# A table of its own for layer B's attention, and every table of orders and steps dealt out anew, in a two-layer encoder kernel

## The chip, the cores and the metric

The kernel runs on one core of one Trainium2 chip. The metric is the device time of one execution in microseconds (us), taken as the median of several executions. Five engines work side by side: TensorE (PE in the profile; its weight loads are PEld), VectorE (DVE), ScalarE (ACT), GpSimd (POOL) and SyncE (SP), which here only issues DMA transfers; POOL issues some too.

## The reference

An input of 256 frames by 2048 features in float32 passes two layers. Cut to what matters:

```python
h = x
u = rms_norm(h, a_norm_g)                      # layer A
q, k, v, fz = split(u @ a_w_in)                # 16 heads of 128
o = forgetting_attention(rms_norm(q), rms_norm(k), v, log_sigmoid(fz + a_b_f))   # causal
h = h + o @ a_w_out
h = h + relu(rms_norm(h, g1) @ w1_A)**2 @ w2_A # d_ff = 8192
kv = rms_norm(h, kv_norm_g) @ kv_w             # keys and values for layer B, computed once
k_sh, v_sh = rms_norm(kv[:, :2048]), kv[:, 2048:]
q = rms_norm(rms_norm(h, b_norm_g) @ b_w_q)    # layer B
o = chunked_relbias_attention(q, k_sh, v_sh, b_rel)   # chunks of 64, own and 8 before
h = h + o @ b_w_out
h = h + relu(rms_norm(h, g2) @ w1_B)**2 @ w2_B
```

All weights are float32 and are read once from memory.

## The kernel before

**Split in two.** A float32 product is made of three products of rounded parts. Each weight block of 128 x 1024 is loaded raw (L295, buffer `raw`, three of them, 1 MB each in the MLPs), ACT rounds it to `hi` (L310), DVE takes the rest as `lo` = raw - hi (L319), and PE multiplies: hi with the activations' high part (L628), hi with their low part (L630), lo with their high part (L632). So every block passes ACT, then DVE, then PE. Four pairs of `hi` and `lo` buffers are there (AHEAD + 2).

**Forms.** The MLPs and layer B's query projection are cut into pairs. An MLP has four chunks of 2048 hidden features, and each chunk has four pairs: `w10`, `w11` (columns of w1) and `w20`, `w21` (columns of w2, which add into the residual `h`). In a pair, part of the contraction is done by seven products of sums instead of eight plain ones: forms f0 to f6, on the weights 11, T3, T2, T1, 21, T4, 22 in this order, each in two halves of 6 matmuls (f0.0 and f0.1 and so on). The rest are plain products: items a4 to a7 and b4 to b7 of 12 matmuls each. The blocks 11 and 12 are brought whole, 1 MB each, into buffers of their own (`bring`, L337, printed w), and turned in place into T3 and T1 by accumulating DMAs that POOL issues (L350). T2 is a sum made on DVE (`make`, L357, tile wT); T4 is T2 plus 21, again on DVE in two halves (L348), and 21 is a raw block, whose buffer is free for the next load when L348 has read it. Between the forms DVE combines accumulators: L673 after f2 (it needs f1's copy p, made by ACT at L671), L675 after f3. f3 writes over the accumulator that L673 reads; a4 and f4 add to the one that it writes.

**Orders and steps.** PE's order is written out in ORDER, one string for each kind of pair, where `r` takes an item that the pair before left over (`first` is the first pair of an MLP, `w20+` and `w21+` are the last two). What the other engines do, and in which order, follows from tables:

- `fetch` (L378) runs before each item: it makes `lo` blocks until LOOK of them are ready, `hi` blocks until MORE further, and loads as far as the raw buffers go.
- BEHIND hangs `make`, `add` (T4 on DVE; T1, T3 as DMAs) and `bring` behind a form; the first number is a delay, counted in `lo` blocks.
- HIDDEN, LONG, SHORT, QUERY, AGAIN, ATT and BIAS say at which step a piece of work is run that belongs to no weight block: `run_fill` takes one step after each item. HIDDEN deals out the squared ReLU of a block of hidden features, LONG and SHORT the norm and transposition of the residual, QUERY and AGAIN layer B's queries and the second use of the turned residual for keys and values, ATT and BIAS an attention group.

A transposition takes DVE's 32 x 32 blocks (L475, tile z) and 16 small DMAs (`moves`, L490, q<-z), eight issued by SP and eight by POOL; ACT then scales the result (L451 for normed inputs, tile y; L990 for hidden features). For heads, `head_norm` squares on ACT (L719) and norms on DVE (L731), the turn goes through memory (land<-turn), and L754 scales what has landed.

At the end `keep_order` fixes the order of DVE, ACT, PE and SP as written; POOL's order is left to the scheduler. A wait thus holds up everything that was written behind it on its engine, SP's transfers included.

The lines that fix it:

```python
def fetch(ahead=AHEAD, early=EARLY, more=0):
    while (units or raws or highs) and len(ready) <= ahead:
        low()
    while (units or raws) and len(ready) + len(highs) <= ahead + more and can_high():
        high()
    while units and sum(r[3] for r in raws) < early:
        load()
    return ready.popleft()
```

Of the kernel before, what the change touches and what calls it, by code (L numbers as in the profile page):

```python
# [29 lines left out]
EARLY = 4  # L30
MINI = 0
HIDDEN = (
# [4 lines left out]
)  # L37
UA = UN // 512
LONG = (
# [4 lines left out]
)  # L44
SHORT = (
# [4 lines left out]
)  # L50
REL = 384
QUERY = (0, 1, 14, 10, 3, 15, 3)
AGAIN = (0, 1, 2, 3, 5, 5, 7, 7)
ATT = ((8, 14, 18, 18, 10), (8, 8, 12, 12, 9))
BIAS = (3, 6, 7)
LOOK = {
# [6 lines left out]
}  # L63
MORE = {
# [6 lines left out]
}  # L71
ORDER = {
# [9 lines left out]
}  # L82
BEHIND = {
    "w10": {(0, 0): [(0, 1, "make", 0), (7, 1, "add", "T1", 0)], (0, 1): [(3, 1, "add", "T1", 1), (0, 1, "make", 1)], (1, 1): [(1, 0, "bring", "12", 0), (1, 0, "bring", "12", 1)], (3, 1): [(6, 0, "bring", "11", 0), (5, 0, "bring", "11", 1)], (4, 0): [(1, 1, "add", "T4", 0)], (4, 1): [(0, 1, "add", "T4", 1), (9, 0, "add", "T3", 1)], (6, 0): [(0, 0, "add", "T3", 0)]},
    "w11": {(0, 0): [(0, 1, "make", 0), (7, 1, "add", "T1", 0)], (0, 1): [(2, 1, "add", "T1", 1), (0, 1, "make", 1)], (1, 1): [(1, 0, "bring", "12", 0), (1, 0, "bring", "12", 1)], (3, 1): [(5, 0, "bring", "11", 0), (7, 0, "bring", "11", 1)], (4, 0): [(0, 1, "add", "T4", 0)], (4, 1): [(0, 1, "add", "T4", 1), (10, 0, "add", "T3", 1)], (6, 0): [(2, 0, "add", "T3", 0)]},
    "w20": {(0, 0): [(7, 1, "add", "T1", 0), (0, 1, "make", 0)], (0, 1): [(0, 1, "make", 1)], (1, 1): [(0, 0, "bring", "12", 0), (0, 0, "bring", "12", 1), (3, 1, "add", "T1", 1)], (3, 1): [(5, 0, "bring", "11", 0), (2, 0, "bring", "11", 1)], (4, 0): [(1, 1, "add", "T4", 0)], (4, 1): [(0, 1, "add", "T4", 1), (8, 0, "add", "T3", 1)], (6, 0): [(0, 0, "add", "T3", 0)]},
    "w21": {(0, 0): [(0, 1, "make", 0), (7, 1, "add", "T1", 0)], (0, 1): [(0, 1, "make", 1), (1, 1, "add", "T1", 1)], (1, 1): [(2, 0, "bring", "12", 1)], (3, 1): [(5, 0, "bring", "11", 0)], (4, 0): [(1, 1, "add", "T4", 0)], (4, 1): [(0, 1, "add", "T4", 1), (9, 0, "add", "T3", 1), (5, 0, "bring", "11", 1)], (5, 0): [(0, 0, "add", "T3", 0)], (2, 1): [(1, 0, "bring", "12", 0)]},
    "q0": {(0, 0): [(0, 1, "make", 0), (7, 1, "add", "T1", 0)], (0, 1): [(3, 1, "add", "T1", 1), (0, 1, "make", 1)], (1, 1): [(1, 0, "bring", "12", 0), (1, 0, "bring", "12", 1)], (3, 1): [(5, 0, "bring", "11", 0), (4, 0, "bring", "11", 1)], (4, 0): [(1, 1, "add", "T4", 0), (0, 0, "add", "T3", 0)], (4, 1): [(0, 1, "add", "T4", 1), (10, 0, "add", "T3", 1)]},
    "q1": {(0, 0): [(0, 1, "make", 0), (8, 1, "add", "T1", 0)], (0, 1): [(5, 1, "add", "T1", 1), (0, 1, "make", 1)], (1, 1): [(1, 0, "bring", "12", 0), (1, 0, "bring", "12", 1)], (3, 1): [(7, 0, "bring", "11", 1), (5, 0, "bring", "11", 0)], (4, 0): [(1, 1, "add", "T4", 0)], (4, 1): [(0, 1, "add", "T4", 1), (10, 0, "add", "T3", 1)], (6, 0): [(0, 0, "add", "T3", 0)]},
}  # L90
SUBS = {"1": (2, 2), "2": (2, 2), "q": (2, 2)}
OPENING = (
    (18, "bring", "12", 0),
    (16, "bring", "12", 1),
    (9, "add", "T3", 0),
    (5, "add", "T3", 1),
    (4, "bring", "11", 0),
    (12, "bring", "11", 1),
)
BIG = 2 * UN  # L100
FORMS = ("11", "T3", "T2", "T1", "21", "T4", "22")
# [14 lines left out]
def trunk(ctx: ExitStack, tc: tile.TileContext, t):  # L116
# [706 lines left out]
    def attend(g, q, k, v, cq, o, make_bias):  # L823
        st = [{} for _ in range(GH)]
        box = {}
        k4 = k.rearrange("p (i a b c) -> p a b i c", i=4, a=GH, b=NB)
        *at, far = ATT[g == NG - 1]
        items = [[] for _ in range(at[-1] + far + 1)]
        step = steps(lambda: make_bias(g, box))
        for i in BIAS:  # L830
            items[i].append(step)
        for a in range(GH):
            step = steps(lambda a=a: softmax(st[a], g, a, q(), k4, box["b"], cq() if cq else None))
            for i in range(4):
                items[at[a] + i].append(step)
            items[at[a] + 3].append(lambda a=a: add_fill(st[a]["carry"]))
            items[at[a] + far].append(lambda a=a: values(st[a], a, v, o, g * GH + a))
        return items
# [220 lines left out]
                            p.evac[q](b, p.ps[q][b])  # L1059

    if MINI:
        for i in range(H):
            o[i] = quarter(i)
            if i % GH == 0:
                G.memset(part[0].bitcast(F32), 0.0)
# [32 lines left out]
    if MINI:  # L1098
        keep_order(tc, (V.engine, S.engine, TE.engine, SY.engine))
        return  # L1100

# [20 lines left out]

    st3, x3, S3 = RowStats("n"), [], []
    stage(o, [next_x(n, None, st3, 4, x3, fs=S3, then=st3.inverse if n == NG - 1 else None) for n in range(NG)], tail=tail_b, plan=plan_b)

    def store(n, r2):
        add_h = residual(n, r2)
# [74 lines left out]
```

## Time and profile before

| | us |
|---|---|
| median of 3 executions | 2114.33 |
| lowest and highest | 2112.9 and 2116.64 |
| the profiled execution | 2111.67 |
| its span, first to last instruction | 2109.9 |
| PE busy | 2073.8 (98%) |
| DVE busy | 1722.0 (82%) |
| ACT busy | 1292.4 (61%) |
| POOL busy | 354.8 (17%) |

The granted TensorE clock was 0.998 over the span, and the kernel moved 538.89 MB at 255 GB/s. In order of time: layer A's projections and attention (to about 340 us), its output projection (to about 386), MLP A (386 to 1053), the query pairs q0 and q1 (1053 to 1141), keys, values and attention of layer B (to 1386), its output projection (to 1430), MLP B (to the end). In the profile a row of a timeline gives start, duration, engine, line, operation, and in brackets how long the engine had been idle and what released it; a matmul row counts several matmuls, and their step is read from the starts of rows that follow each other.

### The profile page before, as it was taken

What the parts mean: (1) busy time and instruction counts of PE and PEld (TensorE: products, weight loads), DVE (VectorE), ACT (ScalarE), POOL (GpSimd) and SP (SyncE); (2) the same over time, 40 slices, a digit from 0 to 9 for tenths busy, and PEclk for the clock granted to TensorE, in tenths of its full rate; (3) what the DMA queues carried; (4) which work ended last, traced back from release to release, by engine and by line L of the source; (5) the groups of instructions that cost most, each with busy time, mean ns of one, the idle gap of its engine ahead of it and who ended that gap; (6) DMA issues with size and microseconds to landing.
All of it is one profiled execution on the core that took longest, in us unless ns stands there. A gap on an engine that the chain in (4) does not pass through costs nothing.

```text
span 2109.9 us, 26958 instructions
## 1 busy us (share of the span) xinstructions
PE 2073.8 (98%) x9114; PEld 1698.1 (80%) x9114; DVE 1722.0 (82%) x2003; ACT 1292.4 (61%) x1567; POOL 354.8 (17%) x552
## 2 busy tenths in 40 slices
PE   9999999999999999999999999999999999999999
PEld 7888888787887887887777888887878878878877
DVE  6777775898889889889998667768988898898896
ACT  6544545676667567567676445456765665675674
POOL 1001001231031022022213001022300310220220
PEclk9999999999999999999999999999999999999999
DMA  8777778899789898888886767778988898888884
GB/s 302 242 257 225 238 245 260 264 263 285 258 267 247 269 285 249 253 276 268 253 246 223 249 212 249 235 249 262 281 272 260 258 263 269 272 254 258 272 262 165
DMA packets 160635, 538.89 MB, mean 255 GB/s; under 512 B 42848, under 2 KB 68080, under 8 KB 125680
## 3 DMA queue, kind: packets, MB, share of 16 engines
q1 hardware_dynamic: 129136, 453.78, 61.1%
q0 software_dynamic: 31360, 83.39, 21.1%
q8 instruction: 71, 1.16, 0.2%
q14 instruction: 68, 0.56, 0.1%
HBM read 497.20 MB, written 15.75 MB: 243 GB/s over the span
## 4 chain that ended last, share of the span: by engine, by line
PE 73%; DMA 10%; DVE 9%; issue 4%; ACT 3%; SPq 1%; DVEq 0%; ACTq 0%; POOL 0%; POOLq 0%
PE acc L628 16%; PE acc L632 16%; PE acc L630 16%; DVE lo L319 6%; PE po L628 4%; PE po L632 4%; PE po L630 4%; PE s L632 3%; PE s L630 3%; PE s L628 3%; DMA w<-in_f2b 2%; DMA w<-in_f2a 2%; ACT hi L310 2%; DMA q<-z 1%; SPq L490 1%
## 5 line engine op out<-in xcount | busy, mean ns | idle before, releaser
L319 DVE TENSOR_TENSOR lo<-raw,hi 128x1024 fp32r<-128x1024 f32 (+1 forms) x634 | 752.8, 1213 | 144.3 <-ACT hi L310 134.3
L310 ACT ACTIVATE hi<-raw 128x1024 fp32r<-128x1024 f32 (+1 forms) x634 | 655.3, 1053 | 309.1 <-PE acc L630 131.5
L628 PE MATMUL acc<-hi,act 128*128 128x512 f32 x1644 | 457.3, 394 | 6.2 <-ACT hi L310 3.3
L632 PE MATMUL acc<-lo,act 128*128 128x512 f32 x1644 | 449.3, 390 | 1.2 <-DVE lo L319 1.2
L630 PE MATMUL acc<-hi,act 128*128 128x512 f32 x1644 | 449.7, 390 | 0.0
L628 PEld LDWEIGHTS acc<-hi,act 128*128 128x128 f32 x1644 | 307.2, 188 | 73.4 <-ACT hi L310 6.6
L632 PEld LDWEIGHTS acc<-lo,act 128*128 128x128 f32 x1644 | 308.3, 188 | 68.1 <-DVE lo L319 3.7
L630 PEld LDWEIGHTS acc<-hi,act 128*128 128x128 f32 x1644 | 309.1, 188 | 65.4 <-DVE act L421 0.5
L310 ACT ACTIVATE hi<-w 128x1024 fp32r<-128x1024 f32 x204 | 210.8, 1054 | 110.6 <-PE po L630 30.3
L319 DVE TENSOR_TENSOR lo<-w,hi 128x1024 fp32r<-128x1024 f32 x204 | 243.5, 1218 | 42.2 <-ACT hi L310 42.0
L490 POOL DMA_DIRECT2D q<-z x336 | 170.4, 529 | 255.2 <-DVE z L475 97.8
L319 DVE TENSOR_TENSOR lo<-wT,hi 128x1024 fp32r<-128x1024 f32 x136 | 161.3, 1218 | 17.7 <-ACT hi L310 17.2
L310 ACT ACTIVATE hi<-wT 128x1024 fp32r<-128x1024 f32 x136 | 141.2, 1052 | 50.7 <-DVE wT L348 26.8
L628 PE MATMUL s<-hi,act 128*128 128x512 f32 x476 | 136.2, 391 | 1.7 <-ACT hi L310 1.6
L630 PE MATMUL s<-hi,act 128*128 128x512 f32 x476 | 135.9, 390 | 0.7 <-DVE act L1001 0.7
L632 PE MATMUL s<-lo,act 128*128 128x512 f32 x476 | 136.0, 390 | 0.6 <-DVE lo L319 0.5
L628 PEld LDWEIGHTS s<-hi,act 128*128 128x128 f32 x476 | 89.4, 188 | 21.7 <-ACT hi L310 2.9
L632 PEld LDWEIGHTS s<-lo,act 128*128 128x128 f32 x476 | 89.1, 188 | 20.4 <-DVE lo L319 1.9
L630 PEld LDWEIGHTS s<-hi,act 128*128 128x128 f32 x476 | 89.2, 188 | 20.2 <-DVE act L1001 1.6
L727 POOL TENSOR_TENSOR rn<-vv,mhalf 128x4 f32<-128x4 f32 x32 | 44.1, 1391 | 341.8 <-DVE vv L726 341.8
L350 POOL DMA_DIRECT2D w<-in_f1a x32 | 28.6, 967 | 324.6 <-ACT hi L310 113.2
L357 DVE TENSOR_TENSOR wT<-w,w 128x1024 f32<-128x1024 f32 x68 | 82.9, 1219 | 0.0
(183 smaller groups left out, 2333.9 us busy)
## 6 DMA issues: line engine op xcount, KB each, us to landing
raw<-in_w_in SPq DMA_DIRECT2D x94, 512.0 KB, 5.2
raw<-in_s1a SPq DMA_DIRECT2D x32, 1024.0 KB, 6.9
raw<-in_s2a SPq DMA_DIRECT2D x32, 1024.0 KB, 7.7
raw<-in_w_kv SPq DMA_DIRECT2D x64, 512.0 KB, 5.8
raw<-in_s1b SPq DMA_DIRECT2D x32, 1024.0 KB, 6.8
raw<-in_s2b SPq DMA_DIRECT2D x32, 1024.0 KB, 5.9
raw<-in_w_oa SPq DMA_DIRECT2D x32, 512.0 KB, 6.1
w<-in_f1a SPq DMA_DIRECT2D x16, 1024.0 KB, 7.0
```

Source lines behind the costliest of these rows:

```text
L310: S.activation(hi[:, c], raw[:, c], AF.Copy)
L319: V.tensor_tensor(lo[:, c], raw[:, c], hi[:, c].bitcast(F32), op=ALU.subtract)
L350: G.dma_start(d, p.big[block][:, half(s)], accum_op=ALU.add)
L357: V.tensor_tensor(p.t["T2"][:, half(s)], p.t["T3"][:, half(s)], p.t["11"][:, half(s)], op=ALU.add)
L490: (SY, G)[j % 2].dma_start(d[32 * j : 32 * j + 32, i], z[32 * i : 32 * i + 32, j * n : (j + 1) * n])
L628: TE.matmul(ps, xh, cut(hi, j), start=first, stop=False, **kw)
L630: TE.matmul(ps, xl, cut(hi, j), start=False, stop=False, **kw)
L632: TE.matmul(ps, xh, cut(lo, j), start=False, stop=last, **kw)
L727: G.tensor_tensor(rn, vv, mhalf, op=ALU.pow)
```

## The change

Every table is given new numbers, ATT and BIAS get entries of their own for layer B (before, both layers used the same), and one line of DMA steps (OPENING) is moved. No instruction of the computation is added or removed. The diff, cut to the entries that the prediction speaks of and the code:

```diff
-QUERY = (0, 1, 14, 10, 3, 15, 3)
-AGAIN = (0, 1, 2, 3, 5, 5, 7, 7)
-ATT = ((8, 14, 18, 18, 10), (8, 8, 12, 12, 9))
-BIAS = (3, 6, 7)
+QUERY = (0, 1, 13, 10, 5, 9, 3)
+AGAIN = (0, 0, 1, 3, 4, 4, 7, 5)
+ATT = ((8, 14, 18, 18, 10), (8, 8, 12, 12, 9), (8, 13, 18, 18, 10), (8, 8, 12, 12, 8))
+BIAS = ((3, 6, 7), (3, 6, 4))
...
 ORDER = {
-    "first": "r f0 r f1 r r r f2 f3 r a a r f4 f6 r b f5 a a b",
+    "first": "r f0 r f1 r r f2 r a f3 a r r f4 f6 r f5 b a a b",
...
-    "w11": "f0 f1 r f2 r r f4 a f3 r a a r r f5 a f6 b b",
-    "w20": "r f0 r f1 f2 f4 r f3 f5 a r a f6 b r r",
+    "w11": "f0 f1 r f2 r r r f4 f3 a a a r r f5 a f6 b b",
+    "w20": "r f0 r f1 f2 f4 r f3 f5 a r r a b f6 r",
...
 BEHIND = {
...
-    "w20": {... (4, 0): [(1, 1, "add", "T4", 0)], (4, 1): [(0, 1, "add", "T4", 1), (8, 0, "add", "T3", 1)], ...},
+    "w20": {... (4, 0): [(2, 1, "add", "T4", 0)], (4, 1): [(0, 1, "add", "T4", 1), (8, 0, "add", "T3", 1)], ...},
...
-        *at, far = ATT[g == NG - 1]
+        *at, far = ATT[2 * (cq is None) + (g == NG - 1)]
...
-        for i in BIAS:
+        for i in BIAS[cq is None]:
```

What moves is read from the instructions' order on each engine. Below, rows with - stand in the kernel before, rows with + in the changed one; the numbers in names like w_5660 only tell buffers apart and differ between the two.

**Pair w20, DVE.** In the pair w20 of the second chunk of MLP A, around f2, f4 and f3 (from 639 us in the trace), DVE's order; the same stands in all eight w20 pairs:

```order
 L319 TENSOR_TENSOR lo<-wT_5427,hi 128x1024 x2
 L319 TENSOR_TENSOR lo<-raw,hi 128x1024 x2
-L348 TENSOR_TENSOR wT_5427<-wT_5427,raw 128x1024 x2
+L348 TENSOR_TENSOR wT_5427<-wT_5427,raw 128x1024
 L673 TENSOR_TENSOR s<-p_5548,po 128x512
-L319 TENSOR_TENSOR lo<-w_5317,hi 128x1024 x2
+L319 TENSOR_TENSOR lo<-w_5300,hi 128x1024
+L348 TENSOR_TENSOR wT_5427<-wT_5427,raw 128x1024
+L319 TENSOR_TENSOR lo<-w_5300,hi 128x1024
 L319 TENSOR_TENSOR lo<-wT_5427,hi 128x1024 x2
 L675 TENSOR_TENSOR po<-po,p_5548 128x512
```

The second half of T4's sum has moved behind L673 and behind one more lo.

**Pair w20, SP.** SP's order in the same pair; w_5660 is block 11 of the pair behind it, w21, and the f in in_f2a marks blocks for the forms, the s those for plain products:

```order
 L490 DMA q<-z 32x256 x8
 L337 DMA w_5505<-in_f2a 128x2048
-L295 DMA raw<-in_f2a 128x2048
-L490 DMA q<-z 32x256 x2
-L295 DMA raw<-in_s2a 128x2048
+L295 DMA raw<-in_s2a 128x2048
+L490 DMA q<-z 32x256 x2
+L295 DMA raw<-in_f2a 128x2048
 L490 DMA q<-z 32x256 x6
 L337 DMA w_5660<-in_f2a 128x2048
```

The two raw loads have changed places; the one right ahead of the six moves is in both cases the one whose buffer L348's second half sets free.

**The first pair of an MLP, ACT.** From the copy p (L671, 386 us in MLP A) on, ACT before:

```order
L671 ACTIVATE p_3433<-po 128x512
L310 ACTIVATE hi<-wT_3309 128x1024
L310 ACTIVATE hi<-w_3228 128x1024 x2
L451 ACTIVATE y<-q,gsb 128x256 x2
L454 ACTIVATE act<-y 128x1024
L310 ACTIVATE hi<-raw 128x1024 x7
L451 ACTIVATE y<-q,gsb 128x256 x4
L454 ACTIVATE act<-y 128x1024
L310 ACTIVATE hi<-wT_3309 128x1024 x2
```

and after:

```order
L671 ACTIVATE p_3433<-po 128x512
L451 ACTIVATE y<-q,gsb 128x256 x2
L454 ACTIVATE act<-y 128x1024
L310 ACTIVATE hi<-wT_3309 128x1024
L310 ACTIVATE hi<-raw 128x1024
L310 ACTIVATE hi<-w_3220 128x1024 x2
L310 ACTIVATE hi<-raw 128x1024 x5
L310 ACTIVATE hi<-wT_3309 128x1024
L451 ACTIVATE y<-q,gsb 128x256 x4
L454 ACTIVATE act<-y 128x1024
L310 ACTIVATE hi<-wT_3309 128x1024
L310 ACTIVATE hi<-raw 128x1024 x4
```

Of the hi blocks before the four L451 one is now of wT_3309 (for f5), and the raw block of b4 stands behind the group; in the kernel before both blocks for f5 stood behind it. The same holds in MLP B.

**Start of the keys and values, ACT.** ACT from the last inputs for keys and values (L451, 1140 us) on, before:

```order
L451 ACTIVATE y<-land,gsb 128x256 x4
L454 ACTIVATE act<-y 128x1024
L310 ACTIVATE hi<-raw 128x1024
L719 ACTIVATE sq<-acc 128x512 x2
L310 ACTIVATE hi<-raw 128x1024
L754 ACTIVATE q<-land,gqk 128x1024
L310 ACTIVATE hi<-raw 128x1024
L754 ACTIVATE q<-land,gqk 128x1024 x2
L310 ACTIVATE hi<-raw 128x1024 x6
L719 ACTIVATE sq<-acc 128x512 x2
L310 ACTIVATE hi<-raw 128x1024 x8
L754 ACTIVATE q<-land,gqk 128x1024
```

and after:

```order
L310 ACTIVATE hi<-raw 128x1024
L451 ACTIVATE y<-land,gsb 128x256 x2
L454 ACTIVATE act<-y 128x1024
L310 ACTIVATE hi<-raw 128x1024
L754 ACTIVATE q<-land,gqk 128x1024
L719 ACTIVATE sq<-acc 128x512 x2
L310 ACTIVATE hi<-raw 128x1024 x2
L754 ACTIVATE q<-land,gqk 128x1024
L310 ACTIVATE hi<-raw 128x1024 x2
L754 ACTIVATE q<-land,gqk 128x1024
L310 ACTIVATE hi<-raw 128x1024 x4
L719 ACTIVATE sq<-acc 128x512 x2
```

The third scaling of queries (L754; the second of the pair printed as x2 before) now stands behind two more hi blocks, and the fourth, below the piece shown, six hi blocks after the third instead of 14. Two of the four L451 have moved up, ahead of the hi block at the head of the second piece.

More of the change, by code (lines that the diff above doesn't have):

```diff
@@ new lines @@
+    "w11": {(0, 0): [(0, 1, "make", 0), (7, 1, "add", "T1", 0)], (0, 1): [(2, 1, "add", "T1", 1), (0, 1, "make", 1)], (1, 1): [(1, 0, "bring", "12", 0), (1, 0, "bring", "12", 1)], (3, 1): [(5, 0, "bring", "11", 0)], (4, 0): [(0, 1, "add", "T4", 0)], (4, 1): [(0, 1, "add", "T4", 1), (9, 0, "add", "T3", 1)], (6, 0): [(1, 0, "add", "T3", 0)], (2, 1): [(7, 0, "bring", "11", 1)]},
+    "w20": {(0, 0): [(7, 1, "add", "T1", 0), (0, 1, "make", 0)], (0, 1): [(0, 1, "make", 1)], (1, 1): [(0, 0, "bring", "12", 0), (1, 0, "bring", "12", 1), (3, 1, "add", "T1", 1)], (3, 1): [(5, 0, "bring", "11", 0), (2, 0, "bring", "11", 1)], (4, 0): [(2, 1, "add", "T4", 0)], (4, 1): [(0, 1, "add", "T4", 1), (8, 0, "add", "T3", 1)], (6, 0): [(0, 0, "add", "T3", 0)]},
@@ new lines @@
+    "w21": {(0, 0): [(0, 1, "make", 0), (6, 1, "add", "T1", 0)], (0, 1): [(0, 1, "make", 1), (0, 1, "add", "T1", 1)], (1, 1): [(2, 0, "bring", "12", 1)], (3, 1): [(5, 0, "bring", "11", 0)], (4, 0): [(1, 1, "add", "T4", 0)], (4, 1): [(0, 1, "add", "T4", 1), (9, 0, "add", "T3", 1), (5, 0, "bring", "11", 1)], (6, 0): [(1, 0, "add", "T3", 0)], (2, 1): [(1, 0, "bring", "12", 0)]},
+    "q0": {(0, 0): [(0, 1, "make", 0), (7, 1, "add", "T1", 0)], (0, 1): [(3, 1, "add", "T1", 1), (0, 1, "make", 1)], (1, 1): [(0, 0, "bring", "12", 0), (1, 0, "bring", "12", 1)], (3, 1): [(5, 0, "bring", "11", 0), (3, 0, "bring", "11", 1)], (4, 0): [(1, 1, "add", "T4", 0), (0, 0, "add", "T3", 0)], (4, 1): [(0, 1, "add", "T4", 1), (10, 0, "add", "T3", 1)]},
@@ L93 @@
     (18, "bring", "12", 0),
-    (16, "bring", "12", 1),
+    (19, "bring", "12", 1),
     (9, "add", "T3", 0),
@@ L97 @@
     (4, "bring", "11", 0),
-    (12, "bring", "11", 1),
+    (14, "bring", "11", 1),
 )
@@ L1061, in trunk @@
     if MINI:
+        V.memset(gqk, 1.0)
         for i in range(H):
@@ L1097, in trunk @@
     st2f = st2.flipped
-    if MINI:
+    if MINI == 1:
         keep_order(tc, (V.engine, S.engine, TE.engine, SY.engine))
@@ L1124, in trunk @@
     stage(o, [next_x(n, None, st3, 4, x3, fs=S3, then=st3.inverse if n == NG - 1 else None) for n in range(NG)], tail=tail_b, plan=plan_b)
+    if MINI == 4:
+        keep_order(tc, (V.engine, S.engine, TE.engine, SY.engine))
+        return
     def store(n, r2):
```

8 lines of the change are left out of this document (2 added, 6 removed), and 44 rows, old and new, of tables (HIDDEN, LONG, LOOK, MORE).

## The prediction

> **What bounds the kernel now.** I read the page first, then the table of windows by stage, PE's waits, and the timelines of each engine around the waits that the change touches.
>
> The page's busy times, and the window of MLP A with the query pairs (us, then busy time of PE, PEld, DVE, ACT and POOL, granted clock, DMA share, GB/s):
>
> ```profile
> PE 2073.8 (98%) x9114; PEld 1698.1 (80%) x9114; DVE 1722.0 (82%) x2003; ACT 1292.4 (61%) x1567; POOL 354.8 (17%) x552
> 382.00:1105.00 723.00, 708.86 (x3085) 577.33 (x3084) 637.88 (x649) 484.33 (x534) 144.79 (x236) 1.00 0.87 264
> ```
>
> PE works nearly all the time, 2073.8 / 9114 = 0.2275 us a matmul, and the change leaves the matmuls as they are. So it can win only PE's waits: 2109.9 - 2073.8 = 36 us in all, 723 - 708.86 = 14 of them here. Behind PE stand DVE (637.88 of 723 us) and the DMA engines (a share of 0.87), both near their own end. PE's waits, summed over the run (us, times, longest):
>
> ```profile
> PE po L628 <- DVE s L673: 11.5, 11, 3.0
> PE acc L632 <- DVE lo L319: 7.3, 13, 0.8
> PE acc L628 <- ACT hi L310: 5.0, 11, 1.7
> PE acc L628 <- DVE qn L731: 1.7, 1, 1.7
> PE pt L615 <- DVE flipper L614: 0.8, 1, 0.8
> ```
>
> The first is f3 waiting for the combination L673: once in q0 (3.0), twice in the first pair of an MLP (1.18 in a row of part 2; I take the same for MLP B, where the order is the same), the other eight in the w20 pairs: 11.5 - 3.0 - 2.36 = 6.1 us. The next two stand at the start of w21, among other places.
>
> **Part 1, the w20 pairs (eight times).** DVE and PE around f3, with the queues:
>
> ```profile
> 643.63 2.35 DVE L348 TENSOR_TENSOR wT<-wT,raw 128x1024 f32<-128x1024 f32 x2
> 645.90 0.69 DVE L673 TENSOR_TENSOR s<-p,po 128x512 f32<-128x512 f32 x1
> 646.50 2.36 DVE L319 TENSOR_TENSOR lo<-w,hi 128x1024 fp32r<-128x1024 f32 x2
> 646.74 0.70 PE L628 MATMUL po<-hi,Sh 128*128 128x512 f32 x2 [0.65 <-DVE s L673]
> 646.06 0.33 SPq L295 DMA_DIRECT2D raw<-in_s2a  x1
> 646.44 4.06 SPq L490 DMA_DIRECT2D q<-z  x6
> 646.75 1.84 POOL L350 DMA_DIRECT2D w<-in_f2a  x2 [3.27 <-ACT hi L310]
> 650.67 0.46 SPq L337 DMA_DIRECT2D w<-in_f2a  x1
> 650.67 10.81 DMA w<-in_f2a
> 661.58 2.01 ACT L310 ACTIVATE hi<-w 128x1024 fp32r<-128x1024 f32 x2 [6.06 <-DMA w<-in_f2a]
> 668.49 0.73 PE L632 MATMUL acc<-lo,Sh 128*128 128x512 f32 x2 [0.62 <-DVE lo L319]
> ```
>
> What goes: with one half of L348 behind it, L673 comes 2.27 / 2 = 1.14 us earlier (643.63 to 645.90 is two halves), more than the 0.65 that f3 waits. What comes: L348's second half ends one L673 (646.50 - 645.90 = 0.60) and one lo (1.14) later, 1.74 in sum. SP stands behind it: the raw load at 646.06 was issued right when L348 was done, and queued behind it are six moves (4.06) and the bring of block 11 for w21 at 650.67. All eight issues come 1.74 later. The bring's own wait, for a lo that ends at 648.86 (646.50 + 2.36), is not what comes last: the same five steps stand before its end after the change, and the bring's turn is at 652.4.
>
> Who waits for the bring: ACT, 6.06 us, and by way of hi and lo PE, 0.62 at 668.49. So the bring's landing sets w21's start, and a w20 that runs 0.65 faster only waits longer there: **the wait that is taken away is worth nothing unless the landing is earlier**, and no step makes it earlier. What counts is whether it gets later. For that I read how busy the DMA engines were (the number before the last):
>
> ```profile
> 646.00:648.00 2.00, 1.35 (x6) 0.90 (x6) 2.00 (x3) 1.22 (x3) 1.25 (x2) 1.00 0.81 177
> 648.00:650.00 2.00, 2.00 (x10) 1.62 (x10) 2.00 (x3) 1.54 (x2) 0.59 (x1) 1.00 1.01 315
> 650.00:656.00 6.00, 6.00 (x28) 4.94 (x27) 6.00 (x6) 3.71 (x4) 0.00 (x0) 1.00 0.99 200
> 656.00:661.50 5.50, 5.50 (x26) 4.55 (x25) 2.54 (x3) 0.00 (x0) 0.00 (x0) 1.00 1.04 381
> 667.80:671.50 3.70, 3.08 (x14) 2.51 (x14) 3.70 (x4) 3.00 (x5) 0.87 (x1) 1.00 1.00 178
> ```
>
> From 648 to the landing at 661.5 they were full, with raw, accumulates, moves and bring. The last row is a stretch with nothing but two accumulates under way, and they fill the engines alone (1.00). The accumulates (646.75) are POOL's and wait for none of this. So if the raw load comes 1.74 later, the accumulates use its time and what is left ends at nearly the same moment. Lost is only the stretch in which neither has data to move: here up to 646.75 - 646.06 = 0.69 us. In the first chunk the accumulate is issued ahead of the raw load, and nothing is lost:
>
> ```profile
> 479.64 1.83 POOL L350 DMA_DIRECT2D w<-in_f2a  x2 [1.97 <-ACT hi L310]
> 480.02 0.33 SPq L295 DMA_DIRECT2D raw<-in_s2a  x1
> ```
>
> Between 0 and 0.69 I take 0.35 later for each pair. The Trainium skill, page "DMA: Bandwidth & Descriptors", section "Queues, rings and completion order", says that each DMA engine goes round the queues that have work for it, a packet at a time; the shares above agree. The same page's section on the anatomy of one DMA puts a transfer at 2.0 us and bytes / 436e3, which is an estimate of 4.4 us for this 1 MB; the trace has 10.81, and the measurement decides.
>
> At w21's start the change also gives a little. Its rows before:
>
> ```profile
> 669.49 1.22 DVE L319 TENSOR_TENSOR lo<-wT,hi 128x1024 fp32r<-128x1024 f32 x1
> 670.62 1.22 DVE L1001 TENSOR_TENSOR act<-q,act 128x1024 fp32r<-128x1024 f32 x1
> 672.24 0.72 PE L628 MATMUL acc<-hi,Sh 128*128 128x512 f32 x2 [0.28 <-ACT hi L310]
> ```
>
> In the new order f2.1's hi stands ahead of the copy L671, and L1001 ahead of f2.0's lo. The 0.28 goes, f2.0's lo comes 1.14 later, and its wait is made up: the net is about -0.25 by these rows. So each pair costs 0.35 - 0.25 = 0.1, and eight cost **+1 us**. The ends: landing unmoved, 8 x -0.25 = -2; landing 1.74 later, 8 x (1.74 - 0.25) = +12.
>
> **Part 2, the first pair of each MLP (twice).** Rows around f3 and f5:
>
> ```profile
> 392.97 0.69 DVE L673 TENSOR_TENSOR s<-p,po 128x512 f32<-128x512 f32 x1
> 393.81 0.70 PE L628 MATMUL po<-hi,S 128*128 128x512 f32 x2 [1.18 <-DVE s L673]
> 406.62 1.71 ACT L451 ACTIVATE y<-q,gsb 128x256 f32<-128x256 f32 x4 [1.28 <-DMA q<-z]
> 409.33 1.99 ACT L310 ACTIVATE hi<-wT 128x1024 fp32r<-128x1024 f32 x2
> 410.42 0.73 PE L628 MATMUL s<-hi,act 128*128 128x512 f32 x2
> ```
>
> a4 now stands between f2 and f3. But a4 adds into the tile that L673 writes, from its third matmul on, so it waits where f3 did: no gain there (ends: -1.2, or +0.6 if the earlier L455 and one more L451 group ahead push L673 back). Then ACT waits at 406.62 for moves to land, works through the L451 group, and only at 409.33 makes the hi blocks of f5. Before, PE had all of b4 to do under that cover and began f5 at 410.42, with 12 matmuls of it to come. After, it has only the first half of f5, and at 410.4, when the next hi is there, half of f5 and b4 are left: 6 matmuls more, 1.37 us, less some 0.2 that PE waited before 410.42. I take +1.2 each, **+2.4 us** (ends 0, if the moves land as much earlier, and 3).
>
> **Part 3, from the queries to the keys and values.** Rows:
>
> ```profile
> 1159.03 1.15 ACT L754 ACTIVATE q<-land,gqk 128x1024 f32<-128x1024 f32 x1 [10.27 <-DMA land<-turn]
> 1161.18 1.20 PE L628 MATMUL acc<-hi,act 128*128 128x512 f32 x4 [1.72 <-ACT hi L310]
> 1142.92 1.23 DVE L455 TENSOR_TENSOR act<-y,act 128x1024 fp32r<-128x1024 f32 x1 [1.18 <-ACT act L454]
> 1147.25 1.22 PE L628 MATMUL acc<-hi,act 128*128 128x512 f32 x2 [1.66 <-DVE qn L731]
> ```
>
> ACT stood 10.27 us at a scaling whose data was still on its way, with the next hi blocks behind it; PE ran dry at 1161.18. With that L754 behind two more hi blocks, PE has 24 matmuls (5.5 us) more before it needs the block behind it: -1.72. The step of the turned residual (L451, L454) comes earlier by two of its four L451, 0.9 us, so L455 at 1142.92 and the norm behind it too: -0.9 of the 1.66. The flip (0.8) wins perhaps half, -0.4. What is late next: nothing in the trace up to 1384. Sum **-3 us** (ends -4 and -1).
>
> **Part 4, the rest.** Layer B's own ATT takes its softmax a step earlier; what can be won is the wait of PE on L820:
>
> ```profile
> PE acc L628 <- ACT act L820: 0.3, 2, 0.2
> ```
>
> I take **-0.4** with the matmul pipeline refilled (ends 0 and -0.5). The eight w11 pairs now run f3 where a4 ran, and f3 needs its lo earlier:
>
> ```profile
> 604.68 1.18 DVE L319 TENSOR_TENSOR lo<-raw,hi 128x1024 fp32r<-128x1024 f32 x1
> 606.95 1.07 PE L632 MATMUL acc<-lo,act 128*128 128x512 f32 x4
> ```
>
> In a4 eight matmuls (1.82) go ahead of the first that uses the lo, in f3 four do (0.91). The lo ends at 605.86, so the cover falls from 606.95 - 605.86 = 1.09 to 1.09 - 0.91 = 0.18. I take nothing; with the cover gone it costs what is missing, and by half a lo in each pair (0.57 - 0.18) it would be +3. The new orders of w10, q0 and q1 move items past each other that PE waits for on neither side, and most entries of HIDDEN, LONG and SHORT move a step between the same blocks: nothing, under the cover of PE's own queue of work.
>
> **The sum.** +1 + 2.4 - 3 - 0.4 = 0.0 us. The profiled execution took 2111.67, 2.66 under the median of 2114.33; against it the forecast is 2111.7, on the median **2114.3 us**. About 0.2%, 4.2 us, is what a measurement of this kernel can tell from no change.
>
> **The rivals.**
>
> *The landing follows the issue (slower).* If a queue's transfers take as long as they did from their issue on, the bring lands 1.74 later in all eight pairs, and the sum is +12 + 2.4 - 3 - 0.4 = +11, 2125.3. For it: the chain that ended last goes straight from the issue at 650.67 into the 10.81 of the transfer. The fit of the skill's page, which counts from the issue, would have it so too. Against it: the full engines. It decides, beyond 0.2%, from a landing about 0.9 later on average: 8 x (0.9 - 0.25) - 1 = 4.2. Chance 0.27.
>
> *The waits taken away are kept (faster).* If w21 is not held by the bring (a landing that comes earlier, because the accumulates end sooner), f3's eight waits are won: -6.1 - 2 + 2.4 - 3 - 0.4 = -9, 2105.3. For it: 6.1 us is what the trace shows. Against it: ACT's 6.06 us of waiting. Chance 0.17.
>
> *It does nothing where it is aimed.* Neither w20 nor the first pair moves PE, and only parts 3 and 4 stay: -3.4, 2110.9. Chance 0.14.
>
> The forecast has 0.42, with a range of its own of 2110 to 2119. The range of 2105 to 2125 takes in the third rival and half of each of the first two. Faster by over 0.2%: 0.17, some of the third and the forecast's lower edge, 0.26. Slower: 0.27 and the upper edge, 0.33. Within: 0.41.
>
> **What would show it.** In the new profile PE's waits on L673 should fall from 11.5 to about 5 us, and ACT's waits for w<-in_f2a and w<-in_f2b grow by as much. In the second chunk the bring of block 11 should be issued about 1.7 us later after L348's first half than it was, and take about 9.4 us instead of 10.81; if it takes 10.8 again, the first rival holds. The 10.27 of L754 should shrink and PE's wait of 1.72 be gone. In the first pair b4 should end near 415, and a6 follow 1.2 later. Wrong I would be if new waits stand in w11 or w10, for which I took nothing.

## The result, and the profile after

The changed kernel takes 2104.55 us (median of 6 executions, 2103.45 to 2107.30), the kernel before, run beside it, 2113.45. The ratio is 0.9957 with an interval of 0.9944 to 0.9970, so it is faster by 9.1 us (6 to 12). The forecast was no change, 2114.3, and the time lies 0.45 us below the lower end of its range. The profiled execution took 2103.45 us, its span is 2101.7, 8.2 less than before. Here and below the ratio is the one that the measurement gives, and it can differ from the ratio of the two medians, most of all in e16 below (-9.1 us by the ratio, -6.2 by the medians).

The page's busy times, and the window of MLP A with the query pairs, the one from the queries to the keys and values, those of attention B and of its output projection, and MLP B (columns as in the prediction):

```profile
PE 2069.0 (98%) x9114; PEld 1696.5 (81%) x9114; DVE 1723.8 (82%) x2003; ACT 1290.3 (61%) x1567; POOL 354.8 (17%) x552
382.00:1105.00 723.00, 710.29 (x3092) 578.43 (x3091) 639.66 (x649) 482.67 (x532) 144.77 (x236) 1.00 0.87 263
1105.00:1160.00 55.00, 50.84 (x222) 40.99 (x221) 46.65 (x61) 37.84 (x51) 21.10 (x25) 1.00 0.66 215
1160.00:1386.00 226.00, 226.00 (x1031) 188.58 (x1031) 154.91 (x260) 108.98 (x175) 14.01 (x14) 1.00 0.74 241
1430.00:2102.00 672.00, 659.20 (x2882) 538.62 (x2881) 579.67 (x581) 431.98 (x456) 120.81 (x196) 1.00 0.84 258
```

PE's waits, summed (us, times, longest):

```profile
PE acc L632 <- DVE lo L319: 8.5, 18, 0.6
PE po L632 <- DVE lo L319: 4.2, 8, 0.6
PE po L628 <- DVE s L673: 2.9, 1, 2.9
PE s L628 <- ACT hi L310: 2.8, 3, 1.6
PE acc L628 <- ACT hi L310: 2.0, 3, 1.2
PE acc L628 <- DVE qn L731: 1.7, 1, 1.7
PE s L628 <- DVE s L673: 1.6, 2, 1.0
PE acc L628 <- DVE acc L675: 0.9, 1, 0.9
```

The wait on L673 has fallen from 11.5 to 2.9 + 1.6 = 4.5, near the 5 that was forecast. But a row stands in its place that was not there: f3's second `lo`, 4.2 us in 8 waits, one in each w20 pair. The seventh row is new, and the fourth has grown (1.6 us in 2 waits before): both by waits in the two first pairs of an MLP, as forecast. In w11 and in the other w10 pairs no wait was added.

Where the time went is read from the starts of the same matmul in both traces. Up to the point in MLP A's first pair where both b4 and f5 are done (413.81 before, 413.79 after) nothing is won, over MLP A 1.2 us (1053.31 and 1052.07), in the query pairs 1.0 is lost (1120.77 and 1120.53), up to the first keys and values 3.4 won (1161.18 and 1157.56), through attention and output projection of layer B 1.4 (1435.30 and 1430.27), in MLP B 3.2. A single pair of traces can't be read finer: executions of one kernel differ by some us. The eight executions profiled of kernels with the old SHORT took between 41.16 and 44.98 us for the same 170 matmuls around MLP A's first pair, and the trace of before is the shortest of them.

The steps that were forecast, in the new trace. The second chunk's w20 pair, DVE, PE and the queue of SP:

```profile
643.62 1.22 DVE L348 TENSOR_TENSOR wT<-wT,raw 128x1024 f32<-128x1024 f32 x1
644.76 0.69 DVE L673 TENSOR_TENSOR s<-p,po 128x512 f32<-128x512 f32 x1
646.49 1.22 DVE L348 TENSOR_TENSOR wT<-wT,raw 128x1024 f32<-128x1024 f32 x1
647.63 1.21 DVE L319 TENSOR_TENSOR lo<-w,hi 128x1024 fp32r<-128x1024 f32 x1
648.89 0.72 PE L632 MATMUL po<-lo,Sh 128*128 128x512 f32 x2 [0.50 <-DVE lo L319]
647.78 0.33 SPq L295 DMA_DIRECT2D raw<-in_f2a  x1
648.16 3.75 SPq L490 DMA_DIRECT2D q<-z  x6
652.08 0.46 SPq L337 DMA_DIRECT2D w<-in_f2a  x1
DMA to landing us min/median/max: 9.7/9.7/9.7
658.16 2.01 ACT L310 ACTIVATE hi<-raw 128x1024 fp32r<-128x1024 f32 x2 [5.49 <-PE s L632]
661.90 2.01 ACT L310 ACTIVATE hi<-w 128x1024 fp32r<-128x1024 f32 x2 [0.78 <-DMA w<-in_f2a]
```

The raw load comes 647.78 - 646.06 = 1.72 later, the bring 1.41 later; it takes 9.7 us (the one DMA of the tile w in that window) instead of 10.81, and lands at 661.8 instead of 661.5. The `lo` behind L348's second half is what f3 now waits for.

From the queries to the keys and values:

```profile
1151.41 1.07 ACT L310 ACTIVATE hi<-raw 128x1024 fp32r<-128x1024 f32 x1 [1.66 <-PE acc L630]
1158.69 1.15 ACT L754 ACTIVATE q<-land,gqk 128x1024 f32<-128x1024 f32 x1 [6.22 <-DMA land<-turn]
1147.01 0.73 PE L628 MATMUL acc<-hi,act 128*128 128x512 f32 x2 [1.66 <-DVE qn L731]
1120.53 1.16 PE L628 MATMUL acc<-hi,act 128*128 128x512 f32 x4 [0.88 <-DVE acc L675]
```

L754 waits 6.22 instead of 10.27, with more hi blocks ahead of it, and PE's 1.72 is gone. The 1.66 on L731 stands as it was, and q1 has a wait of 0.88 that was not there before and that the prediction does not have.

### The profile page after: what moved, and what is told of

Same layout as the page of the kernel before. It is cut to its first block, busy times and chain, and to the rows that moved or that the text cites. A ratio compares the mean times of both kernels' runs of the same rounds, so it can differ in the third digit from the quotient of the medians.

```text
span 2101.7 us, 26998 instructions
## 1 busy us (share of the span) xinstructions
PE 2069.0 (98%) x9114; PEld 1696.5 (81%) x9114; DVE 1723.8 (82%) x2003; ACT 1290.3 (61%) x1567; POOL 354.8 (17%) x552
```

## The experiments

They were run in five sets, each on one chip with the kernel before beside it (medians 2112.5 to 2114.0 there; single executions of it lie between 2106 and 2127). A ratio is turned into us with 2113.7. The tables go in groups: w20, first, query, rest, ATT and SHORT.

**Each group alone, put into the kernel before.** Theory: the sum of the prediction, part by part; the rivals are those of the prediction.

*e1_w20*: all entries of w20.

```diff
-    "w20": "r f0 r f1 f2 f4 r f3 f5 a r a f6 b r r",
+    "w20": "r f0 r f1 f2 f4 r f3 f5 a r r a b f6 r",
-(1, 1): [(0, 0, "bring", "12", 0), (0, 0, "bring", "12", 1), ...], (4, 0): [(1, 1, "add", "T4", 0)]
+(1, 1): [(0, 0, "bring", "12", 0), (1, 0, "bring", "12", 1), ...], (4, 0): [(2, 1, "add", "T4", 0)]
```

> The kernel before, with the changed kernel's entries for the pairs w20 and w20+ alone (order, look-ahead, delays). If the prediction's sum holds for this part: +1 us, and the bring of block 11 lands about 0.35 later. If the landing follows the issue: +12. If the waits of f3 on L673 are kept, as the second rival has it: -6 to -8, which would be nearly all of the 8.9 that the whole change gained. If PE's starts in the two traces are right, where the eight pairs with the start of w21 behind them differ by -2.6 in sum: -2 to -3, and the rest of the gain lies in other tables.

*e2_t4*: of these only the delay of T4's first half.

```diff
-(4, 0): [(1, 1, "add", "T4", 0)]
+(4, 0): [(2, 1, "add", "T4", 0)]
```

> The kernel before, with one number changed: in w20 the first half of T4's sum is delayed by 2 instead of 1, so L673 comes ahead of it. The order of the raw loads stays. Raw load, moves and bring are issued 1.74 later. Landing by the full DMA engines: the bring lands 0 to 0.7 later, takes about 9.4 us instead of 10.8, time within -2 to +2. Landing by issue: bring takes 10.8 again, time +8 to +12. Waits kept: -6.

*e3_first*: the order of the first pair, and OPENING.

```diff
-    "first": "r f0 r f1 r r r f2 f3 r a a r f4 f6 r b f5 a a b",
+    "first": "r f0 r f1 r r f2 r a f3 a r r f4 f6 r f5 b a a b",
-    (16, "bring", "12", 1), ... (12, "bring", "11", 1),
+    (19, "bring", "12", 1), ... (14, "bring", "11", 1),
```

> The kernel before, with the new order of the first pair of an MLP and the new OPENING alone. The prediction's term: +2.4 (b4 no longer under the cover of ACT's wait, 1.2 each). By PE's starts in the two traces: -0.3 in MLP A and +0.8 in MLP B, +0.5 in sum. If f3's waits were won without loss: -2.4.

*e4_query*: QUERY, AGAIN, LONG and the entries of q0 and q1.

```diff
-QUERY = (0, 1, 14, 10, 3, 15, 3)
-AGAIN = (0, 1, 2, 3, 5, 5, 7, 7)
+QUERY = (0, 1, 13, 10, 5, 9, 3)
+AGAIN = (0, 0, 1, 3, 4, 4, 7, 5)
```

> The kernel before, with QUERY, AGAIN, LONG and the entries for q0 and q1 alone. The prediction's term: -3 (1.72 at 1161 us, 0.9 of the wait on qn, 0.4 at the flip). If only the wait at 1161 goes and a new wait stands in q1 (0.88 on L675 in the changed kernel's trace): about -1. If the slower clock after the wait on qn, 1.6 us, goes with the change and not by luck: -2.5 to -3.5, and the clock stays at 1.00 from 1140 to 1160.

*e5_rest*: w10, w11, w21, w21+ and HIDDEN.

```diff
-    "w11": "f0 f1 r f2 r r f4 a f3 r a a r r f5 a f6 b b",
+    "w11": "f0 f1 r f2 r r r f4 f3 a a a r r f5 a f6 b b",
...
```

> The kernel before, with the new entries for w10, w11, w21, w21+ and HIDDEN alone, for which the prediction took nothing. If the parts add up, the three measured ones (w20 +4.0, first pair +3.0, queries -3.4) leave -12.7 of the -9.1 of the whole for this and for ATT, BIAS and SHORT: -8 to -12 here. If the tables only gain together (w21's with w20's, say), it is near 0 or slower here.

*e6_att*: ATT and BIAS with the code that reads them, and SHORT.

```diff
-ATT = ((8, 14, 18, 18, 10), (8, 8, 12, 12, 9))
+ATT = ((8, 14, 18, 18, 10), (8, 8, 12, 12, 9), (8, 13, 18, 18, 10), (8, 8, 12, 12, 8))
 SHORT = (
-    (7, 0, 0, 0, 1, 2, 5, 5, 6, 6),
-    (6, 0, 1, 1, 5, 5, 7, 12, 13, 14),
-    (2, 0, 0, 1, 2, 4, 5, 10),
-    (6, 0, 1, 2, 3, 3, 4, 4),
+    (7, 0, 0, 0, 1, 1, 4, 5, 6, 6),
+    (9, 0, 1, 1, 5, 7, 8, 12, 13, 14),
+    (1, 0, 1, 1, 2, 4, 5, 8),
+    (8, 0, 1, 2, 2, 3, 4, 4),
```

> The kernel before, with layer B's own ATT and BIAS and the new SHORT alone. The prediction's term: -0.4. By PE's starts in the two traces, where three waits between 1384 and 1436 us are gone: -1.3. If the parts add up and the rest is not in w10, w11, w21: down to -12.

| alone | median | ratio, 95% | us | forecast |
|---|---|---|---|---|
| e1_w20 | 2116.30 | 1.0019, 1.0009 to 1.0029 | +4.0 | +1 |
| e2_t4 | 2116.47 | 1.0019, 1.0008 to 1.0029 | +4.0 | as e1 |
| e3_first | 2116.81 | 1.0014, 1.0001 to 1.0028 | +3.0 | +2.4 |
| e4_query | 2110.65 | 0.9984, 0.9973 to 0.9994 | -3.4 | -3 |
| e5_rest | 2113.74 | 0.9999, 0.9987 to 1.0011 | -0.2 | 0 |
| e6_att | 2108.16 | 0.9976, 0.9964 to 0.9988 | -5.1 | -0.4 |

e3, e4 and e5 agree with the forecast within their intervals, and w20's +4.0 lies inside the ends given to it, -2 and 12; e6 is off by 4.7 us. The w20 pairs cost what the one delay of e2 costs (by the medians +2.6 and +2.8), so most likely it is T4 that matters there. The bring's landing, counted from the start of L348's first half and averaged over the eight pairs, is at 17.43 us in before, 17.46 in e3 and 17.42 in e4 with the old order; at 17.78 in e1, 17.48 in e2 and 17.52 in the changed kernel with the new one. The issue is 1.4 to 1.7 us later, the landing 0.05 to 0.35: the landing does not follow the issue. (Over all profiled kernels in which it was read, thirteen with the old order and six with the new one: 17.3 and 17.6.)

**What SHORT does, and what ATT.** In e6 two tables are mixed, so each alone:

> The kernel before with the new SHORT alone. ATT, BIAS and SHORT together gave -5.1. If it is SHORT, which puts the sum L455 ahead of L673 in the first pair of an MLP, so that the transposition (L475), the moves and ACT's group L451 come up to 1.9 us earlier: -4 to -5, with L475 near 392.8 instead of 394.7 and L451 near 404.6 instead of 406.6 us. If it is layer B's attention: 0.

> The kernel before with layer B's own ATT and BIAS alone. The prediction: -0.4, the wait on L820 at 1384 us. If the attention is what gained: -4 to -5. Either way the wait of 0.15 on L820 with its refill, 0.43 in sum, should be gone.

SHORT alone (the rows of SHORT in the diff above) gives 2110.71, 0.9989 (0.9976 to 1.0002), -2.3; ATT and BIAS alone 2112.57, 0.9998 (0.9987 to 1.0010), -0.4, the forecast to the tenth, though the interval of -2.7 to +2.1 can't tell it from nothing; the wait on L820 at 1384 us is gone in its trace. Their sum of -2.7 is just inside e6's interval, -7.6 to -2.5, and SHORT's own interval, -5.1 to +0.4, takes in both nothing and the -4.7 that e6 less e10 gives. What decides for a gain is the traces.

The trace tells where SHORT works. It deals out the steps that end the output projection: the norm and turn of the residual that MLP A's and MLP B's first pairs begin with. ACT around the third block's scaling in before, then in e9:

```profile
382.27 0.91 ACT L451 ACTIVATE y<-q,gsb 128x256 f32<-128x256 f32 x2 [1.23 <-DMA q<-z]
385.93 0.57 ACT L671 ACTIVATE p<-po 128x512 f32<-128x512 f32 x1
```

```profile
380.48 0.91 ACT L451 ACTIVATE y<-q,gsb 128x256 f32<-128x256 f32 x2
384.14 0.57 ACT L671 ACTIVATE p<-po 128x512 f32<-128x512 f32 x1
```

Before, ACT stands 1.23 us for moves with the copy p and the hi blocks of the first pair behind it; with the new SHORT the moves are there and all of it comes 1.8 earlier, the group of four L451 at 405.0 instead of 406.6. The 170 matmuls from 372.65 to 413.81 in before take 41.2 to 45.0 us in eight profiled kernels with the old SHORT (mean 42.7) and 40.0 to 41.2 in nine with the new one (mean 40.5): -2.2. (e13 and e14, with one number of SHORT exchanged, take 41.9 both; the first is among the eight, the second not among the nine.)

Where PE loses this time the trace of before does not show, since it is the shortest of the eight. In the five other kernels with the old SHORT, exactly as it was, and the old order of the first pair PE waits 1.1 to 2.4 us in f5 for a hi that stands behind ACT's group L451; in e10, for one:

```profile
412.96 0.74 PE L628 MATMUL s<-hi,act 128*128 128x512 f32 x2 [1.19 <-ACT hi L310]
```

None of the six kernels with the new SHORT and the old order of the first pair has this wait in MLP A. It is not the moves alone that come earlier there: with the old SHORT ACT also waits for the raw block just ahead of the group (1.86 us in before, 2.8 to 3.0 in e1, e4 and e10), with the new one in e9 it does not wait for that load. How much of the gain goes by the load and how much by the moves is not separated. In layer B the same steps come again, and PE's waits there in before,

```profile
1414.87 1.20 PE L628 MATMUL acc<-hi,act 128*128 128x512 f32 x4 [0.17 <-ACT hi L310]
1435.30 1.21 PE L628 MATMUL acc<-hi,act 128*128 128x512 f32 x4 [0.43 <-ACT hi L310]
1462.05 0.72 PE L628 MATMUL s<-hi,act 128*128 128x512 f32 x2 [0.51 <-ACT hi L310]
```

are all gone in e9. From 1161.18 to 1465.45 the six kernels with the old SHORT and the old order of the first pair take 304.5 us on average, e9 302.0: another -2.5.

**Which row of SHORT.** First the number that I had priced in the prediction, the third row's 10 to 8, which puts L455 ahead of L673; in e13 it alone is new, in e14 the changed kernel has the old one:

```diff
-    (2, 0, 0, 1, 2, 4, 5, 10),
+    (2, 0, 0, 1, 2, 4, 5, 8),
```

> The kernel before with one number of SHORT changed, the last of its third row, 10 to 8. On DVE that moves L455 from behind L673 to ahead of it in the two first pairs and nothing else. If that step is what SHORT gains (-2.3 alone, interval -5.1 to +0.4): -2 to -3, with L475 starting 1.1 to 1.9 us earlier after f2 and PE no longer waiting at f5. If SHORT gains by its other numbers, in the output projections: -0.5 or nothing.

> The changed kernel with that one number put back to 10. In the new order of the first pair f5's second half waits for ACT's group L451 after moves have landed, and L455 back behind a lo and L673 delays the moves. If the step matters: slower than the changed kernel by 2 to 4 (-5 to -7 against before). If not: -9.

e13 takes 2114.93, 1.0004 (0.9989 to 1.0019), +0.9: f3's wait grows from 1.18 to 2.38, and the wait in f5 is gone. e14 takes 2106.87, 0.9964 (0.9951 to 0.9978), -7.6, not to be told from the changed kernel. This number alone is not it. Then the first two rows alone, and the third alone:

> The kernel before with the new first two rows of SHORT only. Theory A (the gain of SHORT is made by its first row, which cuts ACT's group of four L451 on the first turned block in two with a hi block between them): ACT begins that group about 2 us earlier (350.0 instead of 352.2), all that hangs on it up to the third block's moves is issued 1.3 to 2.5 us earlier, ACT's wait of 1.2 to 1.6 us on L451 at 382 is gone, and the whole is 2 to 3 us faster (2111). Rival B (row 3 or row 4 makes it, by bringing the third block's steps nearer): the wait at 382 stays, and the time is that of before within 1 us.

> The kernel before with the new third row of SHORT only. Theory A (row 1 makes the gain): the third block's moves are issued when they were or later, ACT's wait on L451 at 382 stays at 1.2 us or grows, L455 ahead of L673 lengthens f3's wait by 1.2 us, and the time is that of before up to 1 us more (2114 to 2115). Rival B (row 3 makes it): the wait at 382 is gone and the whole is 2 to 3 us faster (2111).

e17 takes 2109.70, 0.9989 (0.9977 to 1.0000), e18 2110.63, 0.9993 (0.9981 to 1.0005): -2.3 and -1.5. Both intervals reach to nothing, but both kernels run the 170 matmuls in 40.6 and 40.5 us, as with the whole of SHORT: each theory's rows do it, and neither theory wins. ACT at the third block, in e17 and in e18:

```profile
381.47 0.91 ACT L451 ACTIVATE y<-q,gsb 128x256 f32<-128x256 f32 x2
```

```profile
381.31 0.91 ACT L451 ACTIVATE y<-q,gsb 128x256 f32<-128x256 f32 x2
```

The wait is gone in both, in two ways. The queue's issues of the third block's first moves, in before, e17 and e18:

```profile
368.74 1.15 SPq L490 DMA_DIRECT2D q<-z  x2
```

```profile
367.91 1.15 SPq L490 DMA_DIRECT2D q<-z  x2
```

```profile
369.10 2.42 SPq L490 DMA_DIRECT2D q<-z  x4
```

In e17 the first block's scaling is cut in two, and the third block's moves are issued earlier, 367.91 instead of 368.74 (1.9 earlier against the matmuls, which stand 1.1 later there in e17). In e18 they are issued later (369.10), but four in a row, with one raw load between the two fours instead of one behind each of the first two pairs, and they land sooner. The DMA view of 364 to 384 us (queue, count, KB each, median us to landing), before and e18:

```profile
q<-z SPq DMA_DIRECT2D x8, 32.0 KB, 5.7
q<-z POOLq DMA_DIRECT2D x8, 32.0 KB, 4.1
```

```profile
q<-z SPq DMA_DIRECT2D x8, 32.0 KB, 3.4
q<-z POOLq DMA_DIRECT2D x8, 32.0 KB, 2.6
```

In e17 these moves take as long as before (6.0 and 4.2). So the wait goes either way; that the load between the moves is what delays them is argued from these rows, what each way is worth the intervals don't tell, and row 4 was not tried alone.

**Do the parts add up?** The new tables without those of the MLPs' pairs, and then each of these put back:

- e11: before, with the diffs of e4 and e6 (all of QUERY, AGAIN, LONG, q0, q1, ATT, BIAS, SHORT new)
- e12: e11 with e3's diff, e15: e11 with e1's, e16: e11 with e5's
- e7: the changed kernel with e1's diff undone, e8: with e3's undone

> The kernel before with the new QUERY, AGAIN, LONG, q0, q1, ATT, BIAS and SHORT, and with the old tables for all MLP pairs. If the parts measured alone add up, -3.4 - 5.1 = -8.5, the whole gain of 9.1 within the interval: then the new orders of the MLP pairs are worth nothing in sum. If the whole needs them: -5 or less.

> The one before this with the first pair's new order and OPENING too. Alone in the kernel before the first pair cost +3.0; taken out of the changed kernel it cost 2.8 (6.3 instead of 9.1 gained). If it gains in company of SHORT: -11, faster than the changed kernel. If it costs wherever it stands: -5.5.

> The kernel with the new QUERY, AGAIN, LONG, q0, q1, ATT, BIAS and SHORT (-8.5), and w20's new entries too. If w20 costs what it cost alone: -4.5. If it is worth the -0.6 by which the changed kernel and its copy with the old w20 differ: -9.

> The same -8.5 kernel with the new entries of w10, w11, w21, w21+ and HIDDEN too; left out against the changed kernel are w20 and the first pair. By the parts alone (-0.2): -8.7. If w20 and the first pair pay only in company with these, this one is slower than -8.5; if they are a burden, it is the fastest.

> The changed kernel with the old entries for w20 and w20+. If w20's new entries cost 4 us wherever they stand, this is the fastest so far: -13 against before. If they cost only in the kernel before and gain in company of the other new tables: slower than the changed kernel, -5 or less.

> The changed kernel with the old order of the first pair and the old OPENING. If the first pair's new order costs 3 us wherever it stands: -12 against before. If it gains with the other tables (PE's starts show -0.3 in MLP A): -8 to -9.

| | median | ratio, 95% | us |
|---|---|---|---|
| e11, no MLP pair | 2104.43 | 0.9960, 0.9946 to 0.9975 | -8.5 |
| e12, + first | 2106.66 | 0.9968, 0.9956 to 0.9980 | -6.8 |
| e15, + w20 | 2108.42 | 0.9973, 0.9961 to 0.9985 | -5.7 |
| e16, + rest | 2107.77 | 0.9957, 0.9938 to 0.9975 | -9.1 |
| e7, first and rest | 2104.77 | 0.9960, 0.9945 to 0.9974 | -8.5 |
| e8, w20 and rest | 2107.55 | 0.9970, 0.9960 to 0.9980 | -6.3 |
| after, all three | 2104.55 | 0.9957, 0.9944 to 0.9970 | -9.1 |

e11 has the whole gain, and it is what e4 and e6 give together: what the diff does to the MLPs' pairs, most of its lines, moves the time by -0.6 us in sum, and the two intervals leave some 4 us either way. In company w20 costs +2.8 (e15 less e11), +2.8 (e8 less e16) and -0.6 (after less e7); first +1.7, +0.6 and -2.8 in the same way. Each of these times has an interval 4 to 8 us wide, and e16's depends most on how the ratio is taken; so neither w20 nor first is shown to cost or to gain in company, and no kernel run here is shown to be faster than the changed one.

That the sum is small does not mean that nothing moved. In w21 (in before the 120 matmuls from 690.42 to 717.68, and their likes in five other chunks) PE stops for a `lo` in some chunks in kernels with the old tables of w10, w11, w21 and HIDDEN: the six stretches take 163.8 to 168.4 us in fourteen of them, 166.3 on average, and 163.2 to 164.7, on average 163.7, in the six with the new ones. These tables gain some 2.7 us there; that alone (e5) they give -0.2 in all speaks for losses elsewhere, but e5's interval of -2.7 to +2.3 does not require them.

Whether first's cost lasts can be read from the starts of the same matmuls, as a tendency only. MLP B's first pair, 1435.30 to 1465.45 us in before, takes 31.0 us on average in the five profiled kernels with the new order and 29.9 in the fifteen with the old one: +1.0, where +1.2 was forecast. The stretch behind it (1465.45 to 1559.37 in before, the rest of that chunk) takes 93.1 and 94.1: -1.1. A w21 pair whose start hangs on a landing would give the time back so. But that stretch spreads from 92.2 to 96.9 over these kernels, far more than what is looked for, and three of the five have the new tables of w21 too: this is possible, not shown.

## Why the prediction was wrong

**The step that failed.** Part 4's sentence on tables, "most entries of HIDDEN, LONG and SHORT move a step between the same blocks: nothing, under the cover of PE's own queue of work", is the step that failed. The order is nearly the same, but where an MLP begins, SHORT's steps are ACT's: ACT waits there for moves, and for a raw block beside them, with the next hi blocks queued behind it, and PE's queue of work does not cover it. With the old SHORT PE stands 1.1 to 2.4 us in f5 in five of six traces, with the new one and the old order of the first pair in none of six. The term should have been -2 to -5: e9 shows -2.3 with an interval that reaches to nothing, e6 less e10 -4.7, and by the starts of the same matmuls e9 is 2.8 shorter than the mean of the six with the old SHORT where MLP A begins and 2.5 shorter around MLP B's. The prediction quoted a wait of the same kind itself, 1.28 us of ACT at 406.62 for q<-z, and priced what the order of `first` would lose under it; it asked neither what SHORT would do to it nor about the one at 382.27. PE's waits in the one trace that it read name neither, because that execution was a lucky one.

**The other part of the miss** is parts 1 and 2. With -4.7 for SHORT, -3.4 for the queries, -0.4 for ATT and -0.6 for the MLPs' pairs the sum is the -9.1 measured; for the MLPs' pairs the forecast was +3.4, 4.0 more. Taken alone, their groups cost +4.0, +3.0 and -0.2. Why that does not come back in company stays open, and the intervals are too wide to say that it is quite gone.

**Part 3 was right in sum.** -3 forecast, -3.4 measured in e4. The 1.72 went as worked out. The 0.9 of the wait on L731 was not won (1.66 before and after), nor the flip (0.9 after, 0.8 before), and a new wait of 0.88 on L675 came in q1. By the starts of the same matmuls, on average over the eleven profiled kernels with the old tables and the nine with the new ones, the stretch from 1120.77 to 1161.18 is 2.9 shorter (40.3 to 37.4) and the one ahead of it, from 1053.31, 1.1 longer. That is -1.8 of the -3.4; the rest is inside e4's interval of -5.7 to -1.3. Some 0.6 of the 2.9 is likely the clock and not the change: the slow matmuls of the last section stand in seven of the eleven and in two of the nine. Part 4's **ATT** agrees in its time, which proves little at this size, and in its mechanism: the wait is gone.

**Part 1's mechanism was right, its price is not explained.** The landing is set by full DMA engines: delayed by 1.4 to 1.7, the transfer takes as much less, and the rival "the landing follows the issue" falls. The accumulates use the time, as forecast: in the second chunk the two land at 651.5 and 657.8 us instead of 655.4 and 658.7. (The row of 667.80 to 671.50 is not accumulates alone, as a bring is issued at 669.60; up to there the share is 1.03, so the reading holds. The shares show full engines, not the order in which they serve the queues.) The Trainium skill, page "DMA: Bandwidth & Descriptors", section "Anatomy of one DMA — SWDGE (gpsimd) path", fits a transfer on GpSimd's path by a fixed time and its bytes alone; this one is issued by SP, and the same 1 MB took 10.81 and 9.7 us with other transfers ahead of it, so the measurement decides. "A w20 that runs 0.65 faster only waits longer there" did not come to be tried, since f3 does not run 0.65 faster: L348's second half now stands ahead of f3's second `lo`, and PE waits 0.50 there. The order rows quoted ahead of the prediction show it, and the sum has no term for it. The forecast that ACT's waits on the bring would grow failed too: for w<-in_f2a and w<-in_f2b together they fall from 37.0 us to 3.5, and of 6.06 us in the second chunk 0.78 is left, because the two hi blocks ahead of it now wait 5.49 us themselves, for PE (the row at 658.16).

Alone w20 costs +4.0 where +1 was forecast, and the missed `lo` is not the reason: with it, f3's waits still fall, from 6.1 us to some 5.0 in e1 and 4.2 in the changed kernel, and the landing moved by about the 0.35 that was put in. The starts don't show where the time goes either: the 720 matmuls from shortly ahead of f3 on, summed over six chunks, take 1003.1 us on average in the six profiled kernels with the new delay of T4 and 1002.7 in the fourteen with the old one, with a spread of 998 to 1007. That cause stays open.

**Part 2 happened as described, but it was priced against a lucky trace.** The new trace of the first pairs:

```profile
393.63 0.73 PE L628 MATMUL s<-hi,act 128*128 128x512 f32 x2 [0.63 <-DVE s L673]
408.99 0.74 PE L628 MATMUL s<-hi,act 128*128 128x512 f32 x2 [0.56 <-ACT hi L310]
413.79 1.07 PE L628 MATMUL s<-hi,act 128*128 128x512 f32 x4
1456.43 0.73 PE L628 MATMUL s<-hi,act 128*128 128x512 f32 x2 [1.56 <-ACT hi L310]
```

a4 waits where f3 did, and PE waits inside f5 for the hi that comes behind the L451 group: 0.56 in MLP A, where SHORT has brought that group 1.4 earlier (405.20), and 1.56 instead of 0.51 in MLP B, +1.05 against the 1.2 forecast. b4 does not end near 415 but at 413.79, where in before f5, then the later of the two, ended (413.81): SHORT has made room for it. In kernels with the new SHORT the new order still costs 0.7 there (170 matmuls in 41.0 us on average over three kernels, 40.2 over the six with the old order). With the old SHORT it costs nothing in MLP A (42.6 in e3, 42.8 on average in the six with the old order), because PE mostly waits in f5 in the old order too, which the trace of before happens not to show; in MLP B it costs 1.1 (31.4 and 30.3). So that e3's +3.0 is near the +2.4 is in part luck.

**The rivals.** "Does nothing where it is aimed" (2110.9) was the nearest in its mechanism: the MLPs' pairs move PE little in sum (-0.6), and parts 3 and 4 as forecast give -3.4, measured -3.8. It lacked SHORT. "The waits taken away are kept" gave 2105.3, nearly the time measured, for a reason that did not occur: f3's waits were replaced, not kept.

## What to carry to other kernels

A table that shifts small steps of a side engine cannot be put at nothing because the work is the same and the wait is not in the bottleneck engine's list: look for every place where that side engine waits for a transfer with the bottleneck's next blocks queued behind it, and ask what reaches it earlier. Read that from more than one trace: the one that was read here was the only one of six in which the bottleneck engine did not wait there for the side engine. Try to issue the moves of one tile together, not with a large load between them. Where many tables change at once, run the groups alone and in company: here most of the diff's lines moved nothing in sum, and groups that cost 3 to 4 us alone are not shown to cost anything together.

## What the runs showed of the hardware

With the DMA engines full, a 1 MB transfer landed within 0.05 to 0.35 us of its old time (means over eight pairs) although it was issued 1.4 to 1.7 later. Eight small moves on SP's queue, 32 KB each, took 3.4 us (median) in e18, issued four, a load, four, instead of 5.7 in before, issued two, a load, two, a load, four. And the clock dips in some executions and not in others: in before, four matmuls right after the wait on L731 take 1.71 us instead of 0.91 (starts of the two rows below), with a granted clock of 0.97 in the window 1105 to 1160, while the changed kernel has 1.00 there and steps of 0.91 after the same wait:

```profile
1148.27 1.91 PE L630 MATMUL acc<-hi,act 128*128 128x512 f32 x4
1149.98 1.30 PE L632 MATMUL acc<-lo,act 128*128 128x512 f32 x4
```

From the matmul that had waited to the tenth behind it that makes 3.87 us instead of 2.39, so some 1.5 us of the difference between the two traces is that. Of the twenty profiled kernels nine have 0.97 in this window, e7 and e16 with the new tables there among them, and e18, with the old ones, has 1.00, so it is not counted to the change.
